# Two-layer hybrid encoder on one core: a second load queue and quarter-wise conversion at the start, a tail without GpSimd

## The chip, the cores and the metric

One NeuronCore of a Trainium2 chip runs the whole program. The metric is device time in microseconds (us) of one execution, as the median of several runs. Names of engines are those of the profile: PE (TensorE matmul), PEld (its weight loads), DVE (VectorE), ACT (ScalarE), POOL (GpSimd), SP (SyncE, which here only issues DMAs).

## What is computed

Two layers over 256 tokens of width 1024, then a last RMSNorm, all in float32:

```python
def hybrid_layer(x, ...):
    h = rms_norm(x, g_mix)
    b_a, c_a, x_a, u_p, q, k, v, ga, gp, gt = split(h @ w_in)
    y_a = short_conv_mixer(...); y_p = multiscale_pool_mixer(...)
    y_t = windowed_gqa(q, k, v, rel_bias, sink) @ w_attn_out
    x = x + (sigmoid(ga)*y_a + sigmoid(gp)*y_p + sigmoid(gt)*y_t) @ w_o
    h2 = rms_norm(x, g_ffn)
    gate, up = split(h2 @ w_gu)
    return x + (silu(gate) * up) @ w_down

def reference(x, ...):
    for layer in range(2): x = hybrid_layer(x, ...)
    return rms_norm(x, g_final)   # y * rsqrt(mean(y*y) + 1e-6) * g
```

## The kernel before

All weights are cut into 128 x 128 blocks and stored in the order of their use (`plan_layer`). A chunk `raw` is 16 blocks (1 MB) and has three buffers; SP loads the chunks one behind the other (`dma_chunk`, L116). Each chunk is converted in halves of 8 blocks (`convert`, L128): ACT copies the half to a rounded high part `hi` (L135), DVE subtracts it from `raw` to give the low part `lo` (L136). `hi` and `lo` have five buffers each. A product of float32 quality is three matmuls (`mm3`, L160 to L164): weight high times x high, weight high times x low, weight low times x high. So a k tile of 4 output tiles takes 12 matmuls.

Activations lie transposed: `x` is 8 tiles of 128 channels x 256 tokens. `xg_tiles` (L241) multiplies x by the norm's gain `ch` and splits it: the high parts on DVE for tiles 0 and 1 (L247) and on ACT for the others (L249), the low parts on DVE (L250). The tokens' norm factor comes later and is applied behind the matmuls: `squares` (L253) lets ACT square x and POOL add the squares up; `norm_stats` (L279) sums them over the channels with tiny matmuls (L282) and computes the factor on ACT and DVE; `norm_rows` (L293) spreads it by four matmuls that wait for `rr` (L289, L290).

The beginning: SP issues, in this order, a quarter of chunk 0 (4 blocks), x tile 0, `ch`, the second quarter, x tile 1, the other half of chunk 0, x tiles 2 and 3, half of chunk 1, x tiles 4 and 5, the other half, x tiles 6 and 7, then whole chunks. Meanwhile PE runs 21 matmuls on zeros (`wps`, L180). The first real product, K and V (`quad_outer`, L327), takes one k tile after the other: 8 k tiles of 12 matmuls, with weights from chunks 0 and 1. Then comes Q (chunk 2 on), with `norm_stats` behind its first output tile and `norm_rows` behind its second.

The end: the last down projection leaves its result in four PSUM banks, two halves of 512 columns (`hh`) for each half of the tokens (`tb`); the bank of (1,1) is finished last. For each, DVE adds the residual (L723) and ACT sums the squares (L725). POOL multiplies the halves `hh` = 1 by the gain `gf` (L729). `rstd` computes the factor with one correction step (L733 to L738), and `store` scales by it, on ACT for `hh` = 1 (L743) and with the gain on DVE for `hh` = 0 (L745), and has SP store the result (L746).

Instructions on each engine run in the order in which the scheduler of the framework put them; an instruction that waits holds up all behind it on its engine.

Of the kernel before, what the change touches and what calls it, by code (L numbers as in the profile page):

```python
# [35 lines left out]
def plan_layer(last):  # L36
    """Order in which the 128 x 128 weight blocks (matrix, k, n) of a layer are used."""
# [53 lines left out]
def trunk(ctx, tc, wst, xT, chp, sinkb, rb, invc, gfin, ident_d, out):  # L91
# [36 lines left out]
    def convert(hc):  # L128
# [4 lines left out]
        for a, b in (((0, 4), (4, 8)) if hc == 0 else ((0, 8),)):  # L133
            s = slice(a * P, b * P)
            S.activation(hi[:, s], raw[:, s], AF.Copy)  # L135
            V.tensor_tensor(lo[:, s], raw[:, s], hi[:, s].bitcast(F32), op=ALU.subtract)  # L136
# [39 lines left out]
    pre0 = const.tile([P, 1], F32, name="pre0")  # L176
    S.activation(pre0, epst, AF.Sqrt)
# [16 lines left out]
    # [0 | I | 0]  # L194
# [8 lines left out]
    # kk[kv]: (high parts of K in both halves of the rows, low parts in one half and zeros in the other)  # L203
# [6 lines left out]
    # vt[key tile]: per pair of KV heads (a, b) the columns [a high | a low | b low | b high]  # L210
# [4 lines left out]
    def build_bias():  # L215
        """stab[h, i] = rel_bias[bucket(255 - i), h] inside the window, NEG outside."""
# [24 lines left out]
    def xg_tiles(l, gi, j, st):  # L241
        """x tiles 2j, 2j+1 times the gain, split."""
        for k in (2 * j, 2 * j + 1):
# [589 lines left out]
```

## Time and profile before

| | |
|---|---|
| median of three runs | 981.03 us (981.01, 981.03, 981.97) |
| profiled execution: span from first to last instruction | 980.1 us |
| median of the runs less that span (no other own time of the profiled execution is given) | 0.9 us |
| PE busy | 968.1 us, 99% of the span |
| DVE, ACT, POOL busy | 715.7, 554.0, 45.7 us |
| last matmul of the program begins | 971.60 us |
| granted PE clock | 0.998 of full speed over the span |

How to read it: PE is busy nearly without a break. Its idle time lies in the first 19 us and in the last 8 us, after the last matmul. Times in the rows below count from the start of the span.

### The profile page before, as it was taken

The numbers are of one execution on the slowest core, as the hardware profiler recorded it, in microseconds if no ns is written. First come the engines' busy times: TensorE is split into PE (matmuls) and PEld (weight loads), VectorE is DVE, ScalarE is ACT, GpSimd is POOL, SyncE is SP. The second block draws the span as 40 slices with busy tenths as digits, with TensorE's granted clock in tenths as the row PEclk, the third lists the DMA queues.
The fourth block names the chain that finished last, engine by engine and source line by source line (L and its number), as shares of the span: only waits on it lengthen the run. The fifth ranks groups of instructions, "written<-read, shape, count | busy, mean of one in ns | idle before, by whom it ended". The sixth has DMA issues, their size and how long they took to land.

```text
span 980.1 us, 19200 instructions
## 1 busy us (share of the span) xinstructions
PE 968.1 (99%) x7877; PEld 954.4 (97%) x7877; DVE 715.7 (73%) x1332; ACT 554.0 (57%) x931; POOL 45.7 (5%) x66
## 2 busy tenths in 40 slices
PE   8999999999999999999999999999999999999996
PEld 7999999999999999999999999999999999999995
DVE  7899898567668955545589898985777697555554
ACT  5866776654456544444477576765554564444443
POOL 5100000000001000000020000000000020000001
PEclk9999999999999999999999999999999999999999
DMA  8755544555554455455443745445554555545531
GB/s 279 254 193 197 189 161 163 197 180 183 189 199 171 174 189 199 173 178 205 178 172 130 248 163 188 161 143 174 192 193 173 172 194 189 200 170 204 184 129 43
DMA packets 27112, 178.12 MB, mean 182 GB/s; under 512 B 3280, under 2 KB 3808, under 8 KB 6800
## 3 DMA queue, kind: packets, MB, share of 16 engines
q1 hardware_dynamic: 24912, 169.93, 49.1%
q0 software_dynamic: 2112, 6.97, 2.5%
q8 instruction: 61, 1.00, 0.4%
q14 instruction: 27, 0.22, 0.1%
HBM read 175.80 MB, written 1.08 MB: 180 GB/s over the span
## 4 chain that ended last, share of the span: by engine, by line
PE 97%; DMA 1%; DVE 1%; SPq 0%; ACT 0%; issue 0%; DVEq 0%; ACTq 0%
PE b L162 25%; PE b L164 25%; PE b L163 25%; PE dn L164 2%; PE dn L162 2%; PE dn L163 2%; PE dn L617 2%; PE dn L616 2%; PE dn L615 2%; PE wo L162 2%; PE wo L163 2%; PE o L389 2%; PE wo L164 2%; PE pt L374 1%; DMA x<-xT 1%; PE sc L348 1%
## 5 line engine op out<-in xcount | busy, mean ns | idle before, releaser
L136 DVE TENSOR_TENSOR lo<-raw,hi 128x1024 fp32r<-128x1024 f32 (+1 forms) x321 | 390.0, 1222 | 215.2 <-ACT hi L135 214.4
L135 ACT ACTIVATE hi<-raw 128x1024 fp32r<-128x1024 f32 (+1 forms) x321 | 337.2, 1055 | 333.1 <-PE b L163 215.0
L162 PE MATMUL b<-h,hi 128*128 128x256 f32 x1344 | 379.8, 283 | 0.0
L164 PE MATMUL b<-h,lo 128*128 128x256 f32 x1344 | 378.4, 282 | 0.0
L163 PE MATMUL b<-h,hi 128*128 128x256 f32 x1344 | 378.3, 281 | 0.0
L162 PEld LDWEIGHTS b<-h,hi 128*128 128x128 f32 x1344 | 253.2, 188 | 0.2
L163 PEld LDWEIGHTS b<-h,hi 128*128 128x128 f32 x1344 | 253.1, 188 | 0.2
L164 PEld LDWEIGHTS b<-h,lo 128*128 128x128 f32 x1344 | 253.1, 188 | 0.0
L163 PE MATMUL b<-xg,hi 128*128 128x256 f32 x448 | 126.6, 283 | 1.6 <-DVE xg L250 1.6
L162 PE MATMUL b<-xg,hi 128*128 128x256 f32 x448 | 126.3, 283 | 1.1 <-DVE xg L247 0.8
L164 PE MATMUL b<-xg,lo 128*128 128x256 f32 x448 | 126.0, 282 | 0.0
L163 PEld LDWEIGHTS b<-xg,hi 128*128 128x128 f32 x448 | 84.4, 188 | 2.3 <-DVE xg L250 2.2
L162 PEld LDWEIGHTS b<-xg,hi 128*128 128x128 f32 x448 | 84.2, 188 | 1.6 <-issue 1.1
L164 PEld LDWEIGHTS b<-xg,lo 128*128 128x128 f32 x448 | 84.4, 188 | 0.0
L164 PE MATMUL dn<-fa,lo 128*128 128x256 f32 x176 | 49.5, 281 | 0.0
L163 PE MATMUL dn<-fa,hi 128*128 128x256 f32 x176 | 49.5, 281 | 0.0
L162 PE MATMUL dn<-fa,hi 128*128 128x256 f32 x176 | 49.5, 281 | 0.0
L260 POOL TENSOR_TENSOR sq<-sq,sq 128x512 f32<-128x512 f32 x12 | 16.2, 1353 | 507.3 <-DVE xg L250 315.5
L358 ACT ACTIVATE s<-s,sm 128x256 f32<-128x256 f32 x64 | 31.8, 500 | 13.0 <-DVE sm L355 13.0
L162 PE MATMUL b<-z,hi 128*128 128x256 f32 x128 | 36.4, 284 | 0.0
L164 PE MATMUL b<-z,lo 128*128 128x256 f32 x128 | 36.1, 282 | 0.0
L164 PE MATMUL b<-ao,lo 128*128 128x256 f32 x128 | 36.0, 282 | 0.0
(174 smaller groups left out, 1537.9 us busy)
## 6 DMA issues: line engine op xcount, KB each, us to landing
raw<-wst SPq DMA_DIRECT2D x158, 1024.0 KB, 4.9
bias<-stab POOLq DMA_DIRECT2D x16, 384.0 KB, 3.9
raw<-wst SPq DMA_DIRECT2D x3, 512.0 KB, 7.7
out<-xn SPq DMA_DIRECT2D x4, 256.0 KB, 2.0
x<-xT SPq DMA_DIRECT2D x3, 256.0 KB, 8.2
raw<-wst SPq DMA_DIRECT2D x2, 256.0 KB, 4.2
gf<-gfin POOLq DMA_DIRECT2D x2, 256.0 KB, 3.8
x<-xT SPq DMA_DIRECT2D x2, 128.0 KB, 4.6
```

The costliest lines, as they stand in the source:

```text
L135: S.activation(hi[:, s], raw[:, s], AF.Copy)
L136: V.tensor_tensor(lo[:, s], raw[:, s], hi[:, s].bitcast(F32), op=ALU.subtract)
L162: PE.matmul(dst, wh, xh, start=start, stop=False, skip_group_check=skip)
L163: PE.matmul(dst, wh, xl, start=False, stop=False, skip_group_check=skip)
L164: last_mm[0] = PE.matmul(dst, wl, xh, start=False, stop=stop, skip_group_check=skip)
L260: G.tensor_tensor(st["acc"], st["acc"], sq, op=ALU.add)
L348: PE.matmul(ps[:, half(j)], qs[t][j][:, cs], kh, start=True, stop=False)
L358: S.activation(s[:, j], s[:, j], AF.Exp, bias=sm[:, 2 + j:3 + j], accum_out=sm[:, 6 + j:7 + j])
L389: PE.matmul(ps[:, half(j)], vv, pts[kt][i][:, half(j)], start=(kt == i == 0), stop=(kt == i == 1))
L615: PE.matmul(d, ah[:, cs], wh, start=(k == 0), stop=False)
L616: PE.matmul(d, ah[:, cs], wl, start=False, stop=False)
L617: PE.matmul(d, al[:, cs], wh, start=False, stop=(k == FT - 1))
```

## The change

At the start, `ch` and the x tiles 0 to 3 are loaded over ACT's queue, which issues them ahead of its first table load; SP is left with the weights and the x tiles 4 to 7. The first four half chunks are converted by quarters, and the x tiles are prepared one by one between them (`convert_first`). The additions of the first norm's squares move from POOL to DVE and stand, in the program, behind all of this; a small POOL copy of their sum takes the place of that sum as what the building of the bias table stands behind. At the end POOL has no work: DVE multiplies by the gain, computes the factor with two instructions in place of a product with two tensors, and scales all four halves by two scalars at once; the last store is issued by ACT.

```diff
@@ dma_chunk
-                nc.sync.dma_start(x[:, xa:xb], xT[:, xa:xb])
-                if c == a == 0:
-                    nc.sync.dma_start(ch, chp)
+                (S if c == 0 else nc.sync).dma_start(x[:, xa:xb], xT[:, xa:xb])
...
+    def convert_first(k):
+        hc, a = k // 2, k % 2 * 4
+        if a == 0:
+            his[hc] = wp.tile([P, HT * P], F32R, name=f"hi{hc}", tag="hi", bufs=5)
+            los[hc] = wp.tile([P, HT * P], F32R, name=f"lo{hc}", tag="lo", bufs=5)
+        s = slice(a * P, (a + 4) * P)
+        raw = raws[hc // 2][:, (hc % 2) * HT * P:(hc % 2 + 1) * HT * P]
+        S.activation(his[hc][:, s], raw[:, s], AF.Copy)
+        V.tensor_tensor(los[hc][:, s], raw[:, s], his[hc][:, s].bitcast(F32), op=ALU.subtract)
...
-    pre0 = const.tile([P, 1], F32, name="pre0")
-    S.activation(pre0, epst, AF.Sqrt)
...
+    S.dma_start(ch, chp)
     dma_chunk(0)
+    pre0 = const.tile([P, 1], F32, name="pre0")
+    S.activation(pre0, epst, AF.Sqrt)
...
-    for j in range(4):
-        convert(j)
-        xg_tiles(0, 0, j, st)
+    for k in range(KT):
+        convert_first(k)
+        xg_tiles(0, 0, k // 2, st, (k,))
     state["cv"] = 4
     for j in range(4):
-        squares(j, st)
-    with tc.issue_after(st["add"].ins):
+        squares(j, st, V)
+    late = const.tile([16, 1], F32, name="late")
+    late_copy = G.tensor_copy(late, st["sum"][:16, 0:1])
+    with tc.issue_after(late_copy.ins):
         build_bias()
...
+            def gain(tb, hh):
+                V.tensor_tensor(xn[2 * tb + hh], xn[2 * tb + hh], gf[hh], op=ALU.mult)
@@ rstd
-                V.scalar_tensor_tensor(fm[:, 4:5], fm[:, 1:2], 1.0 / D, fm[:, 2:3], op0=ALU.mult, op1=ALU.add)
+                V.tensor_scalar(fm[:, 4:5], fm[:, 1:2], 1.0 / D, fm[:, 2:3], op0=ALU.mult, op1=ALU.add)
                 V.reciprocal(fm[:, 5:6], fm[:, 3:4])
-                V.scalar_tensor_tensor(fm[:, 6:7], fm[:, 4:5], fm[:, 5:6], fm[:, 5:6], op0=ALU.mult, op1=ALU.mult)
+                V.tensor_scalar(fm[:, 6:7], fm[:, 4:5], fm[:, 5:6], fm[:, 5:6], op0=ALU.mult, op1=ALU.mult)
                 V.tensor_scalar(fm[:, 7:8], fm[:, 6:7], -0.5, 1.5, op0=ALU.mult, op1=ALU.add)
-                V.tensor_tensor(fm[:, 5:6], fm[:, 5:6], fm[:, 7:8], op=ALU.mult)
@@ store
-                if hh == 1:
-                    S.activation(y, y, AF.Copy, scale=r)
-                else:
-                    V.scalar_tensor_tensor(y, y, r, gf[hh], op0=ALU.mult, op1=ALU.mult)
-                nc.sync.dma_start(out[tb * P:(tb + 1) * P, hh * 512:(hh + 1) * 512], y)
+                V.tensor_scalar(y, y, fm[:, 5:6], fm[:, 7:8], op0=ALU.mult, op1=ALU.mult)
+                q.dma_start(out[tb * P:(tb + 1) * P, hh * 512:(hh + 1) * 512], y)
...
-            sums(0)
-            rstd(0)
-            sums(1)
-            with tc.issue_after(last_add[0].ins):
-                store(0, 0)
-            rstd(1)
-            store(0, 1)
-            store(1, 0)
-            store(1, 1)
+            sums(0, 0)
+            gain(0, 0)
+            sums(0, 1)
+            rstd(0)
+            gain(0, 1)
+            sums(1, 0)
+            store(0, 0, nc.sync)
+            store(0, 1, nc.sync)
+            gain(1, 0)
+            sums(1, 1)
+            gain(1, 1)
+            rstd(1)
+            store(1, 1, nc.sync)
+            store(1, 0, S)
```

Where this puts instructions is set by the scheduler. Three places, all on DVE, which PE waits for in each. The first is the start, from DVE's first instruction that needs loaded data; `xg1` and `xg2` are the parts of x tiles 0 and 1, `lo0` the low half of the first 8 weight blocks. Before:

```order
L136 TENSOR_TENSOR lo0_153<-raw0_105,hi0_152 128x512 [waits DMAHW0_49,Activation_49]
L247 TENSOR_SCALAR xg1_158<-x_103,ch_104 128x256 [waits DMAHW2_49,DMAHW1_49]
L250 SCALAR_TENSOR_TENSOR xg1_158<-x_103,ch_104,xg1_158 128x256 [waits DVE_49]
L247 TENSOR_SCALAR xg2_161<-x_103,ch_104 128x256 [waits DMAHW4_49]
L136 TENSOR_TENSOR lo0_153<-raw0_105,hi0_152 128x512 [waits DMAHW3_49,Activation_49]
L250 SCALAR_TENSOR_TENSOR xg2_161<-x_103,ch_104,xg2_161 128x256 [waits DVE_49]
L136 TENSOR_TENSOR lo1_165<-raw0_105,hi1_164 128x1024 [waits DMAHW5_49,Activation_49]
```

And with the change:

```order
L255 TENSOR_SCALAR xg1_156<-x_101,ch_102 128x256 [waits DMAHW2_49,DMAHW0_49]
L258 SCALAR_TENSOR_TENSOR xg1_156<-x_101,ch_102,xg1_156 128x256 [waits DVE_49]
L255 TENSOR_SCALAR xg2_161<-x_101,ch_102 128x256 [waits DMAHW4_49]
L258 SCALAR_TENSOR_TENSOR xg2_161<-x_101,ch_102,xg2_161 128x256 [waits DVE_49]
L135 TENSOR_TENSOR lo0_153<-raw0_104,hi0_152 128x512 [waits DMAHW1_49,Activation_49]
L135 TENSOR_TENSOR lo0_153<-raw0_104,hi0_152 128x512 [waits DMAHW3_49,Activation_49]
L258 SCALAR_TENSOR_TENSOR xg3_168<-x_101,ch_102,xg3_168 128x256 [waits DMAHW5_49,Activation_49]
L135 TENSOR_TENSOR lo1_165<-raw0_104,hi1_164 128x512 [waits DMAHW6_49,Activation_49]
```

Both x tiles now stand ahead of the first low weights. The second place is DVE between the last x tile (`xg8`) and the norm factor `rr`; `lo4` and `lo8` are the low parts of the first halves of chunks 2 and 4. Before:

```order
L250 SCALAR_TENSOR_TENSOR xg8_191<-x_103,ch_104,xg8_191 128x256 [waits Activation_49]
L136 TENSOR_TENSOR lo4_257<-raw2_118,hi4_256 128x1024 [waits DMAHW3_49,Activation_49]
...
L277 TENSOR_TENSOR nq22_381<-nq22_381 128x2 [waits DVE_49]
L289 CAST rr24_391<-nq22_381 128x2 [waits DVE_49]
L290 TENSOR_TENSOR rr24_391<-nq22_381,rr24_391 128x2 [waits DVE_49]
L136 TENSOR_TENSOR lo8_397<-raw4_312,hi8_396 128x1024 [waits DMAHW5_49,Activation_49]
```

And with the change:

```order
L258 SCALAR_TENSOR_TENSOR xg8_197<-x_101,ch_102,xg8_197 128x256 [waits Activation_49]
L268 TENSOR_TENSOR sq9_200<-sq9_200,sq10_202 128x512 [waits Activation_49]
L268 TENSOR_TENSOR sq9_200<-sq9_200,sq11_205 128x512 [waits DVE_49,Activation_49]
L268 TENSOR_TENSOR sq9_200<-sq9_200,sq12_208 128x512 [waits DVE_49,Activation_49]
L271 TENSOR_TENSOR s113_211<-sq9_200 128x256 [waits DVE_49]
L143 TENSOR_TENSOR lo4_265<-raw2_118,hi4_264 128x1024 [waits DMAHW3_49,Activation_49]
...
L285 TENSOR_TENSOR nq22_389<-nq22_389 128x2 [waits DVE_49]
L143 TENSOR_TENSOR lo8_405<-raw4_320,hi8_404 128x1024 [waits DMAHW5_49,Activation_49]
L297 CAST rr24_399<-nq22_389 128x2 [waits DVE_49]
L298 TENSOR_TENSOR rr24_399<-nq22_389,rr24_399 128x2 [waits DVE_49]
```

Four additions stand ahead of `lo4`, and `lo8`, which needs chunk 4, stands ahead of `rr`. (On ACT the copy to `hi8` moves in the same way ahead of the table load behind the square root.) The third place is DVE at the end, from the addition of the third finished bank (`xn879`, half (1,0)) to that of the last (`xn886`, half (1,1)). Before:

```order
L723 TENSOR_TENSOR xn879_11322<-xn879_11322,dn843_10352 128x512 [waits PE_49]
L734 SCALAR_TENSOR_TENSOR fm903_11997<-fm903_11997 128x1 [waits DVE_49,Activation_49]
L735 RECIPROCAL fm903_11997<-fm903_11997 128x1 [waits Activation_49]
L736 SCALAR_TENSOR_TENSOR fm903_11997<-fm903_11997 128x1 [waits DVE_49]
L737 TENSOR_SCALAR fm903_11997<-fm903_11997 128x1 [waits DVE_49]
L738 TENSOR_TENSOR fm903_11997<-fm903_11997 128x1 [waits DVE_49]
L727 TENSOR_SCALAR fm904_11998<-fm904_11998 128x1 [waits Activation_49]
L723 TENSOR_TENSOR xn886_11491<-xn886_11491,dn844_10353 128x512 [waits PE_49]
```

And with the change:

```order
L733 TENSOR_TENSOR xn879_11330<-xn879_11330,dn843_10360 128x512 [waits PE_49]
L747 TENSOR_SCALAR fm903_12005<-fm903_12005 128x1 [waits DVE_49,Activation_49]
L748 RECIPROCAL fm903_12005<-fm903_12005 128x1 [waits Activation_49]
L741 TENSOR_TENSOR xn872_11161<-xn872_11161,gf1_11154 128x512 [waits DMASW6_49]
L749 TENSOR_SCALAR fm903_12005<-fm903_12005 128x1 [waits DVE_49]
L737 TENSOR_SCALAR fm904_12006<-fm904_12006 128x1 [waits Activation_49]
L741 TENSOR_TENSOR xn879_11330<-xn879_11330,gf0_10983 128x512
L750 TENSOR_SCALAR fm903_12005<-fm903_12005 128x1 [waits DVE_49]
L754 TENSOR_SCALAR xn865_10990<-xn865_10990,fm903_12005 128x512 [waits DVE_49]
L754 TENSOR_SCALAR xn872_11161<-xn872_11161,fm903_12005 128x512
L733 TENSOR_TENSOR xn886_11499<-xn886_11499,dn844_10361 128x512 [waits PE_49]
```

Two products with the gain and two scalings of 512 columns now stand between the two additions. Behind the last addition come the gain of (1,1), the four small instructions of the factor, and the scalings of (1,1) and (1,0).

## Rows read from the trace of the kernel before

**Rows 1.** The page's first part: busy time, share of the span and instructions of each engine.

```profile
PE 968.1 (99%) x7877; PEld 954.4 (97%) x7877; DVE 715.7 (73%) x1332; ACT 554.0 (57%) x931; POOL 45.7 (5%) x66
```

**Rows 2.** What PE waited for over the whole span: total us, times, longest.

```profile
PE b L163 <- DVE xg L250: 1.6, 2, 0.9
PE b L162 <- DVE xg L247: 0.8, 1, 0.8
```

**Rows 3.** Timeline of PE at the start: start us, us, engine, line, operation, count, and in brackets the idle time ahead of it and what ended it. L180 are the matmuls on zeros, L163 at 18.75 is the second matmul of the seventh k tile of K and V, L282 are the sums of the norm, after the first 24 matmuls of Q.

```profile
1.19 4.85 PE L180 MATMUL wps<-warm 128*128 128x256 f32 x21 [1.19 <-DVE epst L175]
...
18.75 0.39 PE L163 MATMUL b<-xg,hi 128*128 128x256 f32 x1 [0.87 <-DVE xg L250]
...
24.31 0.28 PE L164 MATMUL b<-xg,lo 128*128 128x256 f32 x1
24.43 0.50 PE L282 MATMUL ps<-ones,s 128*128 128x1 f32 x4
24.80 0.37 PE L162 MATMUL b<-xg,hi 128*128 128x256 f32 x1
```

**Rows 4.** Stretches of the start: us, PE busy (instructions), granted PE clock, mean busy share of the 16 DMA engines, GB/s.

```profile
3.00:3.50 0.50, 0.50 (x5) 1.00 0.56 143
4.50:5.00 0.50, 0.50 (x5) 1.00 0.79 214
6.00:9.00 3.00, 2.20 (x17) 1.00 1.06 393
9.50:10.50 1.00, 0.69 (x7) 1.00 0.92 141
```

**Rows 5.** Timeline of SP's queue at the start. The first is the first quarter of chunk 0, the second x tile 1, the third the second half of chunk 1, the fourth chunk 2, the last chunk 4.

```profile
0.74 0.39 SPq L120 DMA_DIRECT2D raw<-wst  x1
...
2.60 0.43 SPq L121 DMA_DIRECT2D x<-xT  x1
...
5.81 0.38 SPq L120 DMA_DIRECT2D raw<-wst  x1
...
6.89 0.33 SPq L125 DMA_DIRECT2D raw<-wst  x1
...
17.30 0.33 SPq L125 DMA_DIRECT2D raw<-wst  x1
```

**Rows 6.** Timeline of ACT at the start: first quarter of chunk 0, squares of x tiles 0 and 1, second half of chunk 1, the halves of chunk 2, those of chunk 3.

```profile
4.43 0.63 ACT L135 ACTIVATE hi<-raw 128x512 fp32r<-128x512 f32 x1 [2.19 <-DMA raw<-wst]
...
7.43 0.62 ACT L256 ACTIVATE sq<-x 128x512 f32<-128x512 f32 x1
...
14.32 1.04 ACT L135 ACTIVATE hi<-raw 128x1024 fp32r<-128x1024 f32 x1
...
17.40 2.00 ACT L135 ACTIVATE hi<-raw 128x1024 fp32r<-128x1024 f32 x2 [0.72 <-DMA raw<-wst]
19.95 2.01 ACT L135 ACTIVATE hi<-raw 128x1024 fp32r<-128x1024 f32 x2 [0.54 <-DMA raw<-wst]
```

**Rows 7.** Timeline of DVE at the start: x tile 1 (high), second low quarter of chunk 0, x tile 1 (low), x tiles 2 and 3 (low), and the four low halves of chunks 2 and 3.

```profile
7.26 0.35 DVE L247 TENSOR_SCALAR xg<-x,ch 128x256 fp32r<-128x256 f32 x1
7.56 0.69 DVE L136 TENSOR_TENSOR lo<-raw,hi 128x512 fp32r<-128x512 f32 x1
8.17 0.48 DVE L250 SCALAR_TENSOR_TENSOR xg<-x,ch,xg 128x256 fp32r<-128x256 f32 x1
...
11.19 1.92 DVE L250 SCALAR_TENSOR_TENSOR xg<-x,ch,xg 128x256 fp32r<-128x256 f32 x2
...
19.49 4.62 DVE L136 TENSOR_TENSOR lo<-raw,hi 128x1024 fp32r<-128x1024 f32 x4
```

**Rows 8.** Timeline of the first norm's factor, on ACT (square root of the sums; the halves of chunk 4) and on DVE (the factor's high part `rr`).

```profile
24.97 0.26 ACT L284 ACTIVATE nq<-ps,epst 128x2 f32<-128x2 f32 x1 [3.01 <-PE ps L282]
...
26.65 1.99 ACT L135 ACTIVATE hi<-raw 128x1024 fp32r<-128x1024 f32 x2
...
26.36 0.17 DVE L289 CAST rr<-nq 128x2 fp32r<-128x2 f32 x1
```

**Rows 9.** Timeline of DVE at the end: the last two residual additions, the product L736 for the first and for the second half of the tokens, and the last scaling.

```profile
969.25 0.69 DVE L723 TENSOR_TENSOR xn<-xn,dn 128x512 f32<-128x512 f32 x1 [0.65 <-PE dn L617]
...
970.79 0.22 DVE L736 SCALAR_TENSOR_TENSOR fm<-fm 128x1 f32<-128x1 f32 x1
...
972.02 0.69 DVE L723 TENSOR_TENSOR xn<-xn,dn 128x512 f32<-128x512 f32 x1 [0.57 <-PE dn L617]
...
974.02 0.79 DVE L736 SCALAR_TENSOR_TENSOR fm<-fm 128x1 f32<-128x1 f32 x1
...
975.23 0.75 DVE L745 SCALAR_TENSOR_TENSOR xn<-xn,fm,gf 128x512 f32<-128x512 f32 x1
```

**Rows 10.** Timeline of ACT, POOL and SP's queue at the end: last squares, last square root, the last POOL product, the last two stores.

```profile
972.74 0.63 ACT L725 ACTIVATE dump<-xn 128x512 f32<-128x512 f32 x1 [0.53 <-DVE xn L723]
...
973.50 0.29 ACT L733 ACTIVATE fm<-fm 128x1 f32<-128x1 f32 x1
...
973.54 1.26 POOL L729 TENSOR_TENSOR xn<-xn,gf 128x512 f32<-128x512 f32 x1 [2.88 <-ACT dump L725]
...
976.04 0.81 SPq L746 DMA_DIRECT2D out<-xn  x2
```

**Rows 11.** Groups of DVE instructions by line and shape: busy us, mean ns of one, and idle time ahead.

```profile
L363 DVE TENSOR_SCALAR s<-s,sm 128x256 f32<-128x256 f32 x64 | 19.6, 348 | 0.2
```

More of the change, by code (lines that the diff above doesn't have):

```diff
@@ L132, in convert @@
         lo = wp.tile([P, HT * P], F32R, name=f"lo{hc}", tag="lo", bufs=5)
[L133 to L136, printed above, removed]
+        S.activation(hi, raw, AF.Copy)
+        V.tensor_tensor(lo, raw, hi.bitcast(F32), op=ALU.subtract)
         his[hc], los[hc] = hi, lo
@@ L238, in pair, with xg_tiles @@
         return t[:, 0, :], t[:, 1, :]
-    def xg_tiles(l, gi, j, st):
-        for k in (2 * j, 2 * j + 1):
+    def xg_tiles(l, gi, j, st, ks=None):
+        for k in ks or (2 * j, 2 * j + 1):
             g = ch[:, l, gi, k:k + 1]
@@ L251, in xg_tiles, with squares @@
             st["xg"].append((h, lo))
-    def squares(j, st):
+    def squares(j, st, E):
         sq = tmp.tile([P, 2, T], F32, name=nm("sq"), tag="t2", bufs=8)
@@ L259, in squares @@
         else:
-            G.tensor_tensor(st["acc"], st["acc"], sq, op=ALU.add)
+            E.tensor_tensor(st["acc"], st["acc"], sq, op=ALU.add)
         if j == 3:
             s1 = tmp.tile([P, T], F32, name=nm("s1"), tag="t1", bufs=10)
-            st["add"] = G.tensor_tensor(s1, st["acc"][:, 0], st["acc"][:, 1], op=ALU.add)
+            st["add"] = E.tensor_tensor(s1, st["acc"][:, 0], st["acc"][:, 1], op=ALU.add)
             st["sum"] = s1
@@ L706, in trunk @@
             xg_tiles(l, 1, j, st)
-            squares(j, st)
+            squares(j, st, G)
         acc, xn = ffn(l, st)
@@ L713, in trunk, with sums @@
                 xg_tiles(l + 1, 0, j, st)
-                squares(j, st)
+                squares(j, st, G)
         else:
             fms = [tmp.tile([P, 8], F32, name=nm("fm"), tag="sm", bufs=6) for _ in range(2)]
-            def sums(tb):
+            def sums(tb, hh):
                 fm = fms[tb]
-                for hh in range(2):
-                    y = xn[2 * tb + hh]
-                    last_add[0] = V.tensor_tensor(y, y, acc[2 * tb + hh], op=ALU.add)
-                    dump = tmp.tile([P, 512], F32, name=nm("dump"), tag="t2", bufs=8)
-                    S.activation(dump, y, AF.Square, accum_out=fm[:, hh:hh + 1])
-                    if hh == 0:
-                        V.tensor_scalar(fm[:, 2:3], fm[:, 0:1], 1.0 / D, EPS, op0=ALU.mult, op1=ALU.add)
-                    else:
-                        G.tensor_tensor(y, y, gf[hh], op=ALU.mult)
+                y = xn[2 * tb + hh]
+                add = V.tensor_tensor(y, y, acc[2 * tb + hh], op=ALU.add)
+                dump = tmp.tile([P, 512], F32, name=nm("dump"), tag="t2", bufs=8)
+                S.activation(dump, y, AF.Square, accum_out=fm[:, hh:hh + 1])
+                if hh == 0:
+                    V.tensor_scalar(fm[:, 2:3], fm[:, 0:1], 1.0 / D, EPS, op0=ALU.mult, op1=ALU.add)
+                return add
+            def gain(tb, hh):
+                V.tensor_tensor(xn[2 * tb + hh], xn[2 * tb + hh], gf[hh], op=ALU.mult)
             def rstd(tb):
```

6 lines of the change are left out of this document (2 added, 4 removed).

## The prediction, before the changed kernel had run

> **What bounds the kernel now.** I first read the busy shares. PE works 968.1 of 980.1 us [rows 1], so only its 12 idle microseconds can be won, unless work leaves PE, and the change takes no matmul away. The list of PE's waits then shows where they are not: between the first real matmul and the last it waits for DVE some 2.4 us in all [rows 2], all of it in the first 19 us. So there are two places, the start (until PE runs without a break) and the tail behind the last matmul. Between them every microsecond by which PE is earlier at one instruction is a microsecond of the end, as long as no later wait eats it. I therefore follow one mark: the norm's sums, which PE reaches at 24.43 [rows 3].
>
> The timeline of the start shows who is late. PE's matmuls on zeros end at 6.04; the first product begins when x tile 0 is there, and the last wait ends at 18.75 [rows 3]. In between DVE's low parts are late for two reasons: DVE does halves of 1.22 us ahead of small x tiles, and two x tiles took 1.92 instead of 2 x 0.48 while POOL added squares [rows 7]. The DMA engines are half idle early (0.56 and 0.79), full at 393 GB/s from 6 to 9, and slow at 141 GB/s from 9.5 to 10.5 though 0.92 busy [rows 4]. In the tail the chain is addition, squares, square root, a factor of which one small product takes 0.79 instead of 0.22, scaling, two stores [rows 9, 10]. That product ends with POOL's product (973.54 + 1.26 = 974.80), so it was held by POOL.
>
> **The change at the start.** All times are from the span's start; a DVE instruction that needn't wait starts some 0.08 before the one ahead ends (7.56 + 0.69, next at 8.17 [rows 7]), one that needs its result 0.03 after.
>
> 1. *Loads.* x tile 1 was issued at 2.60 and was there by 7.26, when DVE took it without a wait [rows 5, 7]. It becomes the third on ACT's queue: two issues of 0.46 behind 0.74, so 1.66, or 0.94 earlier. I take 6.3 for its landing. The bounds: 7.2, if the transfer itself is the limit; 5.4, if it needs the 3.7 us of the first load (issued 0.74, used at 4.43 [rows 5, 6]). The four issues delay ACT's table load to about 2.6, its first conversion (4.43) has room for that: nothing.
> 2. *DVE's new order.* x tile 1 costs 0.03 + 0.35 + 0.03 + 0.48, so 7.2; the first low quarter 0.69 less 0.08, so 7.8. PE has done the four matmuls that need only high weights and waits for this quarter: it runs on from 7.83. Behind it DVE needs 2 x 0.61 for weights and 2 x 0.40 for x per two k tiles, 2.0 us, where PE needs 24 x 0.118 = 2.8. ACT's pair takes about the same as DVE's. So with its data there PE runs through: 92 matmuls are left to Q, 92 x 0.118 = 10.9, so Q begins at 18.7. Before, it began 24 x 0.118 ahead of 24.43, at 21.6 [rows 3]. That is 2.9 earlier.
> 3. *Squares on DVE.* They are queued ahead of `lo4`, which PE needs at its third matmul of Q. The second half of chunk 1 was there by 14.32 [rows 6] after an issue at 5.81; SP now has fewer issues ahead and reaches it at about 4.5 (it waits there for the first load's landing at 4.43), so I take 13.0. ACT converts it in two quarters to 14.2, DVE to 15.0, the last two x tiles bring it to 15.8. ACT's last three squares (0.62, 0.54 apart) are done at 16.6. DVE's three additions of 512 columns cost 0.72 each, one behind the other, the last of 256 columns 0.45: 18.3. `lo4` 1.22 [rows 7]: 19.46. PE wanted it at 18.94 and stands 0.5. POOL did the same work beside DVE before, so this is a new wait in place of the one removed.
> 4. Q's first tile then ends at 19.49 + 22 x 0.118 = 22.1: the mark is reached **2.3 us** earlier.
> 5. *The norm's factor.* `lo8` now stands ahead of `rr`, and it needs chunk 4. Sums 22.1, square root read 0.54 later and 0.26 long [rows 3, 8], so ACT is free at 22.9; `hi8` 1.05, `lo8` 1.22, `rr` 0.17: 25.3. PE reaches the matmuls that need it at 22.1 + 0.37 + 24 x 0.118 = 25.3. So nothing is lost if chunk 4 is there at 22.9. Chunks 2 and 3 were used 2.55 us apart (17.40, 19.95 [rows 6]); chunk 4 was issued at 17.30 and used without a wait at 26.65 [rows 5, 8]. With chunk 3 at 19.0, one queue place and some spread behind it, I take 22.3. This has 0.6 us of room, and a late chunk 4 costs its lateness in full.
>
> What else moves costs nothing: the bias table is built behind the POOL copy, from about 18.4 on, when PE has only begun Q, and nothing in the rows waits for it; POOL's additions at the other three norms stay; the matmuls are the same in number.
>
> **The change at the end.** From the third addition at 969.25 [rows 9] DVE now does: addition 0.61, two small 0.21, gain 0.61, two small 0.23, gain 0.61, one small 0.18, two scalings. A scaling of 512 columns by two scalars is not in the trace. A scaling of 256 takes 0.348 [rows 11]. A product takes 0.69 for 512 columns and some 0.53 more for 1024 [rows 7], so 0.27 per 256 columns and 0.16 fixed; 0.348 less 0.16 is 0.19 for 256 columns, nearer to half of 0.27 than to all of it. That gives 0.35 + 0.13 = 0.48, and 0.52 with the second scalar, which I take; the upper end is 0.75, the scaling with a gain [rows 9]. With 0.44 between starts the sum is 3.3: the last addition starts at 972.6 instead of 972.02. The bank waits 0.55 for DVE.
>
> From there: 0.72 + 0.76 to the end of the squares [rows 9, 10], so 974.06; now the gain of (1,1) comes first (0.61; beside it the square root of 0.29 is hidden), then four small ones, 0.76, none of them held by POOL; so 975.43 instead of 975.23. The scalings end at 975.95 and 976.39. Stores were issued at 976.04 and about 976.42 [rows 10]; now at 975.98 on SP and 976.42 on ACT. **The tail gives 0.0**: what the shorter chain and POOL's absence save (0.57 for the held product, 0.2 for the one dropped) goes into the late addition and the gain. Bounds: 0.1 better with scalings of 0.48; with 0.75, 0.23 more for each of four, 0.9 worse.
>
> **Sum.** 2.3 + 0.0. The profiled execution spans 980.1; the median 981.03 lies 0.9 above, which I leave as it is. Span 977.8, time **978.7 us**, 0.24% less. A measurement of this kernel can tell about 0.2%, 1.96 us, from no change; so "faster" begins below 979.07, close to the forecast.
>
> **Rivals.**
>
> *The second queue brings nothing* (0.17). For it: the engines show 0.79 to 1.06 from 4.5 on, and packets were slow from 9.5 to 10.5 with the engines at 0.92 [rows 4], so what lies behind may come when it came before. Then x tile 1 lands at 6.3 to 7.2 and the second half of chunk 1 at 14.3; step 3 ends at 20.7, PE stands 1 us more, and the mark gains 1.1, or 0.6 with all loads as late as before: 980.2. Against it: 0.56 and 143 GB/s from 3.0 to 3.5, when one queue alone was feeding them. The Trainium skill says in DMA: Bandwidth & Descriptors, section Issuing engines are not separate DMA queues, that DMAs from several engines run on the same 16 DMA engines and that spreading them saves only the sequencer's issue time. By that rule this rival holds; the early half-idle rows do not agree with it fully, since there issue and not transfer looks like the limit.
>
> *The loads come sooner still* (0.13): the slow stretch from 9.5 to 11.5 is an accident and the same bytes land a further 1 us earlier. Then `lo4` is there in time, no 0.5 is lost, x tile 1 comes 0.4 earlier: gain 3.2, 977.8.
>
> *DVE becomes the bound of the tail* (0.08): scalings at 0.75 each, 0.9 us: 979.6. For it: all POOL's and ACT's work of the tail is now in one queue. The chain of waits would show the last addition start behind a scaling at about 973.0.
>
> *Slower: `rr` behind a late chunk 4* (0.04). One mechanism, `lo8` in DVE's queue. The factor is ready 2.45 us after chunk 4's landing, PE came to it at 27.64 before (24.80 + 24 x 0.118); so from a landing at 25.2 on the whole gain is gone. Chunk 2 took 10.5 us from issue to use (6.89, 17.40 [rows 5, 6]); chunk 4 issued at 15.4 with 10.5 lands at 25.9: 0.7 lost, 981.7. Slower by over 0.2% needs 27.2. Against it: chunk 2 had 3 MB queued ahead, chunk 4 has one.
>
> *The change does not do what it says*: the framework could have kept the squares between the quarters. The order on DVE shows that it did not; no chance is kept for it.
>
> **How the numbers follow.** The forecast has 0.58, with a range of its own from 978.0 to 979.4 (x tile 1 between 5.8 and 6.8, chunk 1 half a microsecond either way, scalings 0.48 to 0.62). The whole range, 977.5 to 980.5, takes in the second queue's failure and most of the two smaller rivals. Faster by over 0.2%: about four fifths of the forecast's 0.58 and the sooner loads, 0.61. Slower by over 0.2%: 0.02. The rest, 0.37, is within.
>
> **What would show it.** Right: K and V start at 6.1, PE stands once until 7.8 and once at the third matmul of Q for about half a microsecond, for `lo4` behind the squares; the sums come at 22.1; `rr` is in time; the last addition starts at 972.6 less 2.3 with PE long done, and the small factor instructions take 0.15 to 0.25. Wrong: x tile 1 past 7, `hi3` or `hi4` waiting for DMA past 14.3 and 17.4, a wait of PE for `rr`, or scalings of 0.7.

## The result, and the profile after

The changed kernel takes **983.74 us** (median of ten runs, 982.86 to 984.95) against 981.65 before (ten runs, 981.01 to 982.23): a ratio of 1.0023, 95% interval 1.0014 to 1.0031. It is slower by 0.23%. The forecast was 978.7 with a range up to 980.5.

The profiled execution spans 981.2, one of the shorter of the ten (their spans have a median of 982.0). The page gives PE about the busy time that it had in [rows 1], so nothing was added to PE's work:

```profile
PE 968.6 (99%) x7877; PEld 955.5 (97%) x7877; DVE 716.2 (73%) x1343; ACT 552.0 (56%) x932; POOL 38.0 (4%) x61
```

PE's waits over the whole span, to be set against [rows 2]:

```profile
PE b L171 <- DVE lo L135: 2.2, 1, 2.2
...
PE b L169 <- DVE xg L255: 1.0, 1, 1.0
```

Before, PE waited 2.4 us for x tiles in three waits. Of these only the one for x tile 0 is left, longer than before (1.0 against 0.8), and a wait of 2.2 for a low quarter of the weights (L135) stands in place of the others. PE's timeline says when (columns as in [rows 3]; L290 are the sums, the mark of the prediction):

```profile
7.08 0.35 PE L169 MATMUL b<-xg,hi 128*128 128x256 f32 x1 [1.03 <-DVE xg L255]
...
7.85 0.28 PE L170 MATMUL b<-xg,hi 128*128 128x256 f32 x1
10.31 0.58 PE L171 MATMUL b<-xg,lo 128*128 128x256 f32 x1 [2.18 <-DVE lo L135]
...
13.25 0.41 PE L171 MATMUL b<-xg,lo 128*128 128x256 f32 x1
13.46 0.31 PE L169 MATMUL b<-xg,hi 128*128 128x256 f32 x1
...
25.59 0.50 PE L290 MATMUL ps<-ones,s 128*128 128x1 f32 x4
```

Four matmuls run, as predicted; then PE stands until 10.31, where the prediction had 7.83. From there 15 matmuls take 3.3 us until 13.6, some 0.21 apart, and only later ones are 0.118 apart. From the sums on the two run alike: the last matmul starts 947.1 behind them, before 947.2. The stretches show why (us, PE busy, granted clock, DMA share, GB/s, as in [rows 4]):

```profile
6.00:9.00 3.00, 1.02 (x5) 1.00 1.02 384
9.50:10.50 1.00, 0.19 (x1) 0.80 1.00 365
10.50:12.50 2.00, 2.00 (x10) 0.50 1.07 426
...
13.50:14.50 1.00, 1.00 (x10) 0.99 1.15 426
```

PE was busy for 1.02 of the 3 us from 6 to 9 (2.20 before, [rows 4]) and hardly from 9.5 on; then the granted clock falls to 0.50 (1.2 instead of 2.4 GHz), just as the matmuls start. The wait behind all this is told by DVE's timeline at the start (against [rows 7]; in order the high part of x tile 0, that of x tile 1, two low quarters, the squares, the first four low halves of chunks 2 and 3):

```profile
6.58 0.35 DVE L255 TENSOR_SCALAR xg<-x,ch 128x256 fp32r<-128x256 f32 x1 [3.74 <-DMA x<-xT]
...
8.78 0.35 DVE L255 TENSOR_SCALAR xg<-x,ch 128x256 fp32r<-128x256 f32 x1 [1.33 <-DMA x<-xT]
...
9.57 1.29 DVE L135 TENSOR_TENSOR lo<-raw,hi 128x512 fp32r<-128x512 f32 x2
...
17.64 2.28 DVE L268 TENSOR_TENSOR sq<-sq,sq 128x512 f32<-128x512 f32 x3
...
20.29 4.63 DVE L143 TENSOR_TENSOR lo<-raw,hi 128x1024 fp32r<-128x1024 f32 x4
```

x tile 1 was there at 8.76, and DVE stood for it with the low quarter queued behind it. Before, it was taken at 7.26 without a wait [rows 7]. Yet it had been issued sooner, as ACT's own rows show (the queue's issues, then the first conversion):

```profile
0.74 0.41 ACTq L188 DMA_DIRECT2D ch<-chp  x1
1.19 1.42 ACTq L121 DMA_DIRECT2D x<-xT  x3
...
5.15 0.63 ACT L134 ACTIVATE hi<-raw 128x512 fp32r<-128x512 f32 x1 [1.02 <-DMA raw<-wst]
```

The second of the three x issues is 1.67 after the start, and the load took 7.1 us. The first weight quarter, too, was converted at 5.15 instead of 4.43 [rows 6]. The packets of the stretch from 6.0 to 7.5 tell where the time went. Each line is a queue: packets, MB, and their time as a share of the 16 engines. First the kernel after (q1 is SP's queue, q10 ACT's), then the kernel before:

```profile
DMA packets 258, 0.59 MB, mean 395 GB/s; under 512 B 38, under 2 KB 129, under 8 KB 258
...
q1 hardware_dynamic: 112, 0.41, 66.3%
q10 hardware_dynamic: 114, 0.12, 23.0%
```

```profile
DMA packets 254, 0.59 MB, mean 395 GB/s; under 512 B 40, under 2 KB 113, under 8 KB 254
...
q1 hardware_dynamic: 216, 0.57, 97.7%
```

The bytes are the same, 0.59 MB. After, the two queues have as many packets each, 112 and 114, but SP's carry 3.7 KB and ACT's 1.1 KB. For each small packet of x a large one of weights now goes through the engines.

The norm's factor was just in time: `rr` ends on DVE at 28.87, and PE takes it without a wait at 28.91. In the tail (DVE, then SP's and ACT's last issues, against [rows 9, 10]; PE's last matmul starts at 972.70, before 971.60):

```profile
972.77 1.00 DVE L754 TENSOR_SCALAR xn<-xn,fm 128x512 f32<-128x512 f32 x2
973.69 0.68 DVE L733 TENSOR_TENSOR xn<-xn,dn 128x512 f32<-128x512 f32 x1
975.15 0.69 DVE L741 TENSOR_TENSOR xn<-xn,gf 128x512 f32<-128x512 f32 x1 [0.79 <-ACT dump L735]
...
976.08 0.27 DVE L749 TENSOR_SCALAR fm<-fm 128x1 f32<-128x1 f32 x1
...
976.57 1.00 DVE L754 TENSOR_SCALAR xn<-xn,fm 128x512 f32<-128x512 f32 x2
```

```profile
977.15 0.33 SPq L755 DMA_DIRECT2D out<-xn  x1
```

```profile
977.61 0.35 ACTq L755 DMA_DIRECT2D out<-xn  x1
```

The last addition starts 0.99 after the last matmul's start, before 0.42: 0.57 late, behind two scalings. The product that POOL had held (0.79 in [rows 9]) takes 0.27. From the last matmul's start to the span's end it is 8.5, before and after.

### The profile page after: what moved, and what is told of

It is laid out like the page before. It is cut to its first block, busy times and chain, and to the rows that moved or that the text cites. A ratio compares the mean times of both kernels' runs of the same rounds, so it can differ in the third digit from the quotient of the medians.

```text
span 981.2 us, 19201 instructions
## 1 busy us (share of the span) xinstructions
PE 968.6 (99%) x7877; PEld 955.5 (97%) x7877; DVE 716.2 (73%) x1343; ACT 552.0 (56%) x932; POOL 38.0 (4%) x61
## 4 chain that ended last, share of the span: by engine, by line
PE 98%; DMA 1%; DVE 1%; issue 0%; ACTq 0%; ACT 0%; DVEq 0%
PE b L171 25%; PE b L169 25%; PE b L170 25%; PE dn L170 2%; PE dn L169 2%; PE dn L171 2%; PE dn L625 2%; PE dn L624 2%; PE dn L623 2%; PE wo L169 2%; PE wo L170 2%; PE o L397 2%; PE wo L171 2%; PE pt L382 1%; PE sc L356 1%; PE sc L357 1%
## 5 line engine op out<-in xcount | busy, mean ns | idle before, releaser
L143 DVE TENSOR_TENSOR lo<-raw,hi 128x1024 fp32r<-128x1024 f32 x316 | 385.4, 1227 | 211.4 <-ACT hi L142 210.5
L142 ACT ACTIVATE hi<-raw 128x1024 fp32r<-128x1024 f32 x316 | 332.7, 1058 | 326.4 <-PE b L170 215.9
L169 PE MATMUL b<-ao,hi 128*128 128x256 f32 x128 | 36.0, 281 | 0.0
```

Source lines behind the costliest of these rows:

```text
L142: S.activation(hi, raw, AF.Copy)
L143: V.tensor_tensor(lo, raw, hi.bitcast(F32), op=ALU.subtract)
L169: PE.matmul(dst, wh, xh, start=start, stop=False, skip_group_check=skip)
```

## The experiments

The forecast failed at the start, so the theory to test was: **x tile 1 comes late because it shares the engines packet by packet with the weights, the first low quarter waits behind it on DVE, and PE's gap costs the clock as well.** The rivals: the second queue costs time outside the span, DVE's order alone is wrong, the tail loses. Times are medians of 8 to 11 runs beside the kernel before on the same chip (981.74 to 981.85), with the ratio to it and its 95% interval; spans and marks are of one profiled execution each. An interval reaches some 0.9 us to either side, so a difference of less than some 1.3 between two of these kernels is not clear by the times alone and rests on the profiled executions.

**One queue** (`a2_all_sp`). All loads and stores back on SP in the old order:

```diff
-                (S if c == 0 else nc.sync).dma_start(x[:, xa:xb], xT[:, xa:xb])
+                nc.sync.dma_start(x[:, xa:xb], xT[:, xa:xb])
+                if c == a == 0:
+                    nc.sync.dma_start(ch, chp)
...
-    S.dma_start(ch, chp)
...
-            store(1, 0, S)
+            store(1, 0, nc.sync)
```

> The changed kernel with every load and store back on SP's queue, in the order of before (first quarter, x tile 0, ch, second quarter, x tile 1, ...); quarters, squares on DVE and the new tail stay. With one queue the scheduler also puts the first low quarter back ahead of x tile 1 on DVE. Theory A (loads on two queues share the 16 DMA engines, so x tile 1 comes late behind big weight packets, PE idles and its clock falls; and a second hardware queue adds about 0.9 us outside the span): x tile 1 is there by 7.3, the granted clock stays 1.00, the norm's sums come at about 23.4 instead of 25.6, span about 979 and time minus span back at 0.9: 980.0 to 980.8 us, faster than before. Rival B (the squares on DVE, lo8 ahead of rr, or the tail's DVE queue make it slow): still 983 or slower, sums later than 24.4.

Measured: 980.07, ratio 0.9981 (0.9973 to 0.9990), 3.7 below the change; x tile 1 is taken at 7.01. The time is as theory A had it, its account of the start is not: the profiled execution, the slowest of the eleven (981.79), has the sums at 24.67 instead of 23.4. PE waits there 1.4 for x tile 2 and then runs at a granted clock of 0.50 until 15.0, where theory A had 1.00; and time less span is 1.8, not 0.9. `g1_add_first` below has the same start, and its profiled execution the sums at 22.82: marks of one execution can be that far apart. The framework also put the first low quarter ahead of x tile 1 again and the squares between the quarters, so this is two edits in one. The next two part them, as far as x tile 1 and the first two low quarters go.

**The order alone** (`d1_low_first`): two queues, but the low quarters ahead of x tile 1.

```diff
-        convert_first(k)
-        xg_tiles(0, 0, k // 2, st, (k,))
+        low = convert_first(k)
+        if k == 0:
+            low0 = low
+        if k == 1:
+            with tc.issue_after(low0.ins):
+                xg_tiles(0, 0, 0, st, (k,))
...
```

> The changed kernel with the two low quarters of the first weights ahead of x tile 1 on DVE; loads on two queues as in the change. Theory A (PE idles because the low quarter is queued behind an x tile that lands at 8.8): PE does the whole first k tile at about 7.1 to 9, then waits for x tile 1 until about 9.2 and for x tile 2 until about 11.3, the clock stays 1.00, the sums come at about 23.2 instead of 25.6: 2.4 us faster than the changed kernel, about 981.3, with about 1.8 outside the span. Rival (loads alone set the time): the sums stay at 25 or later, 983.5.

Measured: 981.11, ratio 0.9993 (0.9985 to 1.0002). x tile 1 comes as late as in the change (taken at 8.87), and the sums are at 23.67. Theory A held but for the clock, which falls here too (0.51 from 9 to 12). The framework also set the later quarters and x tiles by turns, one by one.

**The queue alone** (`e1_queue_only`): the edit of `a2_all_sp`, and the change's order on DVE kept by hand up to the second low quarter, with the squares behind the last x tile:

```diff
+    convert_first(0, 1)
+    convert_first(1, 1)
+    xg_tiles(0, 0, 0, st)
+    with tc.issue_after(last_lo[0].ins):
+        low0 = convert_first(0, 2)
+    with tc.issue_after(low0.ins):
+        convert_first(1, 2)
...
+        with tc.issue_after(last_lo[0].ins):
+            squares(j, st, V)
```

> The change with all loads and stores on SP's queue, in the order of before, while VectorE keeps the order of the change (both small x tiles ahead of the first low quarter, the squares behind the last quarter). Theory A (the second queue is what is wrong: it delays x tile 1 and everything queued behind it): x tile 1 is taken at 7.0 to 7.3, the first low quarter ends at 8.5, PE's wait for it is 1.5 to 1.9 instead of 2.2 and ends near 8.5 instead of 10.3; the sums come at 24.0 to 24.3 and the time is 980.3 to 981.0. Rival B (the order on VectorE is what is wrong, whatever the queue): the time stays at 982.5 or above, since the low quarter still stands behind an x tile.

Measured: 981.40, ratio 0.9997 (0.9988 to 1.0005), sums at 24.25. DVE's rows show x tile 1 without a wait and the low quarter at once behind it:

```profile
7.33 0.35 DVE L259 TENSOR_SCALAR xg<-x,ch 128x256 fp32r<-128x256 f32 x1
7.72 0.49 DVE L262 SCALAR_TENSOR_TENSOR xg<-x,ch,xg 128x256 fp32r<-128x256 f32 x1
8.12 2.61 DVE L140 TENSOR_TENSOR lo<-raw,hi 128x512 fp32r<-128x512 f32 x4
```

PE's wait for it is 1.0 and ends at 8.86, not 10.31. The sums come in theory A's range although the clock falls here too (0.59 from 9 to 12); the time is 0.4 above its upper end, and what makes the 0.4 was not tried. So rival B fell, and the four kernels make a table (in the last one the squares stand between the quarters too):

| | x tile 1 ahead of the low quarter | low quarter first |
|---|---|---|
| x tiles and gains on ACT's queue | 983.74 | 981.11 |
| all on SP's queue | 981.40 | 980.07 |

Undoing either gives back 2.3 to 2.6, undoing both 3.7: each costs more because of the other.

**Packets in turn or bytes in turn** (`i1_x01_one_transfer`): x tiles 0 and 1 as one transfer, so half as many packets of twice the size.

```diff
-            for a, b, xa, xb in (((0, 4, 0, 1), (4, 8, 1, 2), (8, 16, 2, 4)), ((0, 8, 4, 6), (8, 16, 6, 8)))[c]:
+            for a, b, xa, xb in (((0, 4, 0, 2), (4, 8, 2, 2), (8, 16, 2, 4)), ((0, 8, 4, 6), (8, 16, 6, 8)))[c]:
...
-                (S if c == 0 else nc.sync).dma_start(x[:, xa:xb], xT[:, xa:xb])
+                if xb > xa: (S if c == 0 else nc.sync).dma_start(x[:, xa:xb], xT[:, xa:xb])
```

> The change with x tiles 0 and 1 as one transfer on ACT's queue (128 packets of 2 KB in place of 256 of 1 KB; the first additions of squares move between the weight quarters with it). Theory A (the engines take packets from the two queues in turn, so a queue of small packets gets a small share of the bytes): both tiles are there at 7.0 to 7.5, x tile 1 some 1.5 earlier than 8.78 and x tile 0 some 0.5 later than 6.58; the first low quarter ends at about 9.4 instead of 10.2, PE's long wait ends there, and the time is 982.8. Rival B (the two queues share by bytes, or ACT's queue starts late): both tiles at 8.5 or later, the low quarter at 11 and the time 984.4.

Measured: 982.32, ratio 1.0008 (0.9999 to 1.0017), 1.4 below the change. The packets from 6.0 to 7.5 and DVE's first rows:

```profile
q1 hardware_dynamic: 98, 0.36, 58.7%
q10 hardware_dynamic: 102, 0.19, 35.8%
```

```profile
7.33 0.62 DVE L255 TENSOR_SCALAR xg<-x,ch 128x256 fp32r<-128x256 f32 x2 [4.49 <-DMA x<-xT]
7.86 0.88 DVE L258 SCALAR_TENSOR_TENSOR xg<-x,ch,xg 128x256 fp32r<-128x256 f32 x2
8.65 1.29 DVE L135 TENSOR_TENSOR lo<-raw,hi 128x512 fp32r<-128x512 f32 x2
```

As many packets on either queue again, and ACT's share of the bytes went from 0.12 to 0.19 MB. x tile 1 comes 1.45 earlier, x tile 0 0.75 later, as theory A said; rival B had both at 8.5 or later. The issue of x tile 1, 0.48 sooner with one transfer less, can't make 1.45. So turns by packets are the reading that fits, and this is why x tile 1 was late. Little of it reaches the sums in this execution, the slowest of its eleven: PE goes on at 9.39 instead of 10.31, but its matmuls are 0.21 apart until 13.8, and the sums come at 25.37 instead of 25.59.

**The clock.** The change once more, for a second profile (`after_again`):

> The change once more, unaltered, for a second profile. The medians of ten runs (span 982.0) and the profiled execution (span 981.2) differ by 0.8. Theory A (the granted clock falls at the start in every execution, for a time that differs): x tile 1 at 8.6 to 9.0 again, PE's wait for the low quarter about 2.2, matmuls 0.21 apart for 3 to 5 us behind it, sums at 25.6 to 26.5. Rival B (the first profile was an accident): x tile 1 before 8.0 and no fall of the clock.

Measured: one run, 984.61, span 982.6. x tile 1 is taken at 8.77 and PE waits 2.2 for the low quarter and goes on at 10.30, all within 0.04 of the first profile, yet the sums come at 26.83 instead of 25.59. Stretches as above:

```profile
9.50:10.50 1.00, 0.20 (x1) 0.50 0.90 293
10.50:14.50 4.00, 4.00 (x19) 0.50 1.05 426
14.50:16.50 2.00, 2.00 (x12) 0.55 1.00 385
```

Here the half clock lasts until 16.3, not 13.5. The loads repeat within 0.04; the length of the slow stretch does not, and it makes most of the 1.4 between the two spans. Then `c1_warm51`, the change with 51 matmuls on zeros:

```diff
-WARM = 21
+WARM = 51
```

> The changed kernel with 51 instead of 21 matmuls on zeros, so that PE has work until about 9.9 us and the wait for the first low quarter is short. Theory A: the granted clock stays 1.00 through the start, the 15 matmuls from 10.3 on go at 0.118 instead of 0.21 us, which is 1.4 us, less up to 0.4 for the four real matmuls that now stand behind the zeros: about 1 us faster than the changed kernel, 982.7. Rival (the clock does not matter, the loads set the time): no gain, 983.7 or a little more.

Measured: 983.03, ratio 1.0012 (1.0003 to 1.0021), 0.7 below the change. The products run 0.118 apart from 10.5 on, the sums come at 24.58. But PE's waits show what is late next:

```profile
PE b L171 <- DVE lo L135: 0.9, 1, 0.9
PE ps L306 <- DVE rr L297: 0.7, 2, 0.5
```

The factor `rr` is late by 0.2 here and by 0.5 at the same norm of the second layer, so part of the gain is given back; in the two profiled executions all of it (the last matmul starts at 972.89, in the change at 972.70). It is the queue of my smallest rival, low halves ahead of `rr` on DVE (six in a row until 27.4 here, one more than the change has there), but not its late chunk 4: ACT converted `hi8` without a wait by 23.4. The interval of this time overlaps that of the change. And `d2_low_first_warm30`, `d1_low_first` with 30 matmuls on zeros (`WARM = 30`):

> The change with the low quarters ahead of x tile 1 and 30 matmuls on zeros instead of 21, so that PE works on until the first product. Theory A (the fall of the granted clock behind PE's early gaps costs its 15 matmuls at half rate in full): the clock stays at 1.00, the sums come at about 22.4, time 979.8. Rival B (the fall is mostly hidden, since x tile 2 is ready only at 11.9 and PE would wait for it): the clock stays at 1.00, PE waits about 1 us for x tile 2, the sums come at 23.3 and the time is 980.8. Rival C (the clock falls all the same): 981.1, no change from 21 matmuls.

Measured: 981.06, no change from `d1_low_first` (981.11); matmuls 0.118 apart from 8.2 on, sums at 23.53. Rival B held: with the clock up PE stands from about 11.2 for x tile 2, which ACT has at 11.6. Here the fallen clock cost only time that PE would have waited for data anyway.

**Time outside the span** (`b1_before_act_store`): the kernel before, with only its last store on ACT's queue.

```diff
-            def store(tb, hh):
+            def store(tb, hh, q=nc.sync):
...
-                nc.sync.dma_start(out[tb * P:(tb + 1) * P, hh * 512:(hh + 1) * 512], y)
+                q.dma_start(out[tb * P:(tb + 1) * P, hh * 512:(hh + 1) * 512], y)
...
-            store(1, 1)
+            store(1, 1, S)
```

> The kernel before, with only its very last store issued by ACT instead of SP. Theory A (what lies outside the span grew from 0.9 to 1.8 us because a second hardware queue is used at all): span as before within 0.3, time about 0.9 us more, 982.5 us. Rival B (the 0.9 comes from something else in the changed kernel, such as the loads at its start): same as before, 981.6.

Measured: 981.85, ratio 1.0001 (0.9992 to 1.0010). Time less span is 1.8 (1.7 to 2.1) in the runs of this kernel, of the change and of all others. A second queue costs nothing there.

**The tail.** The kernel before with the change's end alone, once with the last store on ACT's queue (`t1_tail_only`), once with all four on SP's (`t2_tail_sp`):

```diff
-            store(1, 0, S)
+            store(1, 0, nc.sync)
```

> The kernel before with the change's end alone (one store on ACT's queue with it). Theory A (the prediction's step on the tail, 0.0): 981.8 within 0.3, from the last matmul's start to the span's end 8.5 us as before, and the last addition begins 0.9 to 1.0 after the last matmul's start instead of 0.42. Rival B (part of the change's loss is in the tail): 982.3 or above. Rival C (the tail gains what leaving POOL out saves, 0.5 to 0.8): 981.2 or below.

> The kernel before with the change's end, all four stores on SP. Theory A (a transfer on a queue of ACT that has not been used before lands 0.8 to 1.0 later, as 3.2 against 2.1 to 2.3 in the runs so far, and this alone made the end by itself slower): the last store lands 2.1 after its issue, from the last matmul's start to the span's end 8.2, time 981.5. Rival B (the end's chain of operations is slower by itself): tail 9.0 or more and time 982.5.

Measured: 982.66, ratio 1.0008 (0.9999 to 1.0017), against 981.44, ratio 0.9998 (0.9989 to 1.0006). The first is above its theory A's range, where rival B had it; the second came as its theory A said. From the last matmul's start to the span's end it is 9.2 and 8.4. DVE does the same in both; the stores differ (KB, us from issue to landing), here of `t1_tail_only`, of the change, and of `t2_tail_sp`:

```profile
out<-xn ACTq DMA_DIRECT2D x1, 256.0 KB, 3.2
```

```profile
out<-xn ACTq DMA_DIRECT2D x1, 256.0 KB, 2.2
```

```profile
out<-xn SPq DMA_DIRECT2D x2, 256.0 KB, 2.2
```

The store on ACT's queue takes 1.0 longer where it is that queue's first transfer; in `b1_before_act_store` it took 3.0. In the change the queue has carried loads, and it takes 2.2. So the end by itself is worth about nothing (0.3 less in time with SP's stores, inside the interval), and the longer tail of `t1_tail_only` is not in the change.

**The late addition** (`g1_add_first`): `a2_all_sp` with the last addition ahead of the two scalings.

```diff
-            store(0, 0, nc.sync)
-            store(0, 1, nc.sync)
             gain(1, 0)
-            sums(1, 1)
+            last = sums(1, 1)
+            with tc.issue_after(last.ins):
+                store(0, 0, nc.sync)
+                store(0, 1, nc.sync)
```

> The kernel with all loads and stores on SP, and the last addition ahead of the two scalings of the first token block. Theory A (the two scalings hold the last addition by 0.57, the step on the tail had the mechanism right): the addition begins 0.42 after the last matmul's start, the tail is 8.0 instead of 8.5 and the time 979.5, 0.5 below the same kernel without it. Rival B (the gain that follows is then held by the scalings, or the stores are later): tail 8.4 to 8.5, time 980.0.

Measured: **979.47**, ratio 0.9974 (0.9964 to 0.9985), 0.6 below `a2_all_sp` (the intervals overlap), and 0.26% faster than before: the lowest time here. DVE's tail (PE's last matmul starts at 969.95):

```profile
970.38 0.69 DVE L734 TENSOR_TENSOR xn<-xn,dn 128x512 f32<-128x512 f32 x1 [0.39 <-PE dn L626]
970.98 0.99 DVE L755 TENSOR_SCALAR xn<-xn,fm 128x512 f32<-128x512 f32 x2
971.89 0.68 DVE L742 TENSOR_TENSOR xn<-xn,gf 128x512 f32<-128x512 f32 x1
```

The addition starts 0.43 after the last matmul's start again, and the tail is 7.75 instead of the 8.2 of `a2_all_sp`: 0.45, which the tail's own rows show.

**A smaller use of the second queue** (`h1_best_x0_ch_on_act`): `g1_add_first` with only the gains and x tile 0 on ACT's queue.

```diff
-                nc.sync.dma_start(x[:, xa:xb], xT[:, xa:xb])
-                if c == a == 0:
-                    nc.sync.dma_start(ch, chp)
+                (S if c == a == 0 else nc.sync).dma_start(x[:, xa:xb], xT[:, xa:xb])
...
+    S.dma_start(ch, chp)
```

> The kernel with one queue and the last addition ahead of the scalings (979.5), with only the gains and x tile 0 on ACT's queue, so that SP is two issues of 0.46 ahead with all else. Theory A (issue time is what is left to win, and 180 KB on the second queue disturb little): x tile 1 at 6.7 to 7.1, the second half of chunk 0 at 8.2 to 8.6, the sums 0.3 to 0.9 earlier than 22.8, time 978.6 to 979.2. Rival B (the early loads are bound by the engines, not by issue): 979.5. Rival C (x tile 0 is delayed by taking turns with the weights): x tile 0 at 6.6 or later, time 979.9 or above.

Measured: 981.03, ratio 0.9992 (0.9983 to 1.0001), 1.6 above `g1_add_first`. x tile 0 is taken at 6.64 (6.29 in `g1_add_first`, 5.73 in `a2_all_sp`), so rival C held: even 180 KB on the second queue come later there than in SP's own. But the 1.6 are not the queue's alone: the framework also put the first low quarters behind x tile 0 on DVE (from 7.43; in `g1_add_first` the first runs at 5.27, ahead of it). The clock does not part the two, since in both PE's first products are 0.21 apart (until 11.3 here, 10.4 there).

## Why the prediction was wrong

It failed at its **step 1**, the landing of x tile 1: 6.3, with bounds 5.4 to 7.2. It landed at 8.76, outside them. I took the time of issue for what held the load, since one queue left the engines half idle early on [rows 4], and bounded the landing above by what it had been before. A transfer moved to another queue did not keep its place, however: it took turns with whatever the first queue carried, packet for packet. `i1_x01_one_transfer` bears that out, and `e1_queue_only`, with x tile 1 back in SP's queue, has it at 7.33.

The Trainium skill states this rule in DMA: Bandwidth & Descriptors, section Queues, rings and completion order: a DMA engine goes round the queues that have work, packet by packet. The trace agrees, with 112 and 114 packets of the profile's count; how many of these make one turn it does not show. I had weighed another section of that page, by which the second queue brings nothing (chance 0.17, 980.2). That was the right direction, but no rival of mine let the queue make a load later.

From there, by the prediction's own steps:

- *Step 2, the low quarter ready at 7.8 and PE on from 7.83*: the order on DVE was as told, and it turned the late tile into a late quarter. PE went on at 10.31, 2.5 later. That PE "runs through" at 0.118 was the second error: 15 matmuls at the granted clock of 0.50 took 3.3 instead of 1.8, 1.5 more. Nothing in my sum priced a gap of PE beyond its length; `c1_warm51`, which fills that gap with matmuls on zeros, has no slow matmuls behind it.
- *Step 3, 0.5 for `lo4` behind the squares*: no wait, as PE came so late; `lo4` was done at 21.5.
- *Step 4, the mark at 22.1*: 25.59. The parts give 2.5 + 1.5 − 0.5 = 3.5, which is the difference. In place of 2.3 earlier it was 1.2 later.
- *Step 5, `rr` in time*: right, with 0.04 to spare. Where PE came earlier `rr` was 0.2 late in `c1_warm51` and `d1_low_first` and in time in `d2_low_first_warm30`, so the gain I forecast could have met it.
- *The tail, 0.0*: right, 8.5 before and after. The addition 0.57 late (predicted 0.55), two scalings in 1.00 (0.96), the small product 0.27 (0.2). The 0.0 hid 0.5 that could be had, as `g1_add_first` shows.
- *The sum*: I set the span of 980.1 against the median 981.03 and left 0.9 between them. The time is 1.7 to 2.1 above the span in every run, so the profiled execution was the one of 981.97, and even with every step right I should have said 979.6. The account closes: 0.9 here, 3.5 at the mark, and 0.8 because the median execution is longer than the profiled one, make 5.2; the miss is 5.0. That the 0.8 is the length of the half clock is not shown; the two profiles of the change and its ten mean clocks (0.996 in the two shortest executions, 0.994 or 0.995 in the five longest) suggest it.

What I had right were the order on DVE and the length of the tail. What stays open is which packets bring the gains and x tile 0 late in `h1_best_x0_ch_on_act` and how much of its loss is the order on DVE, and why the slow clock lasts until 13.5 in one execution and 16.3 in another with the same loads.

## What to carry to other kernels

Before a small urgent load goes to a second queue, count the packets: it takes turns with the first queue's packets, so small ones lose against large ones, and issue time saved is no landing time saved. Where work is reordered so that a quarter of the weights stands behind such a load, bound its lateness by a landing later than today's too, and price an early gap of PE by the clock as well as by its length. Set a sum made in a profiled execution against that execution's own time, not against the median.

## What the runs showed of the hardware

**The same stretch moved more with the x tiles on ACT's queue, but not only while two queues ran side by side.** From 9 to 12 us, PE busy, granted clock, DMA share, GB/s, of the kernel before and of the change:

```profile
9.00:12.00 3.00, 1.94 (x14) 1.00 0.99 221
```

```profile
9.00:12.00 3.00, 1.69 (x8) 0.68 1.04 393
```

`e1_queue_only` has 221 and `d1_low_first` 398, and the engines count as busy in all four. But from 10.5 to 12 SP's queue is alone in both kernels; packets, MB and share, before and after:

```profile
q1 hardware_dynamic: 147, 0.36, 95.4%
```

```profile
q1 hardware_dynamic: 222, 0.64, 106.8%
```

One queue moves 0.64 MB there, where before it moved 0.36, and with one queue at work its packets can be slow or fast. Why they are slow in the kernel before was not tried. The faster loads came too late to help the change: its first small ones, on which PE waited, had landed behind weights by then.

**The granted clock does not always show the slow start.** In `g1_add_first` PE's first products, and the stretch around them:

```profile
7.81 0.41 PE L171 MATMUL b<-xg,hi 128*128 128x256 f32 x1
8.02 0.41 PE L172 MATMUL b<-xg,hi 128*128 128x256 f32 x1
```

```profile
6.50:10.50 4.00, 3.71 (x17) 1.00 1.05 355
```

They are 0.21 apart until 10.4, as elsewhere at 0.50, while the row says 1.00. The same is so in `i1_x01_one_transfer` until 13.8 and in `t2_tail_sp` until 10.3, and for the matmuls on zeros of the kernel before: 21 in 4.85 us, 0.23 each [rows 3], where the rows say 1.00 [rows 4]. The spacing of matmuls is the surer sign. The Trainium skill, in TensorE: Matmul & The Clock Gate, section Seeing it yourself, warns that records of the clock gate are not always reliable; this row agrees.

**The first transfer on ACT's queue was slow.** 3.0 and 3.2 us for a store of 256 KB on ACT's queue that had carried nothing (two kernels), 2.2 on the same queue in the change, 2.0 to 2.3 on SP's.
